# Hymba encoder layer, one core: neighbourhood attention in slots of two heads, with three score banks and three projection banks

## The chip, the cores and the metric

One core of a Trainium2 chip. The metric is the device time of one execution, in microseconds (us), from start to end on that core. The engines are TensorE (PE in the profile; PEld are its weight loads), VectorE (DVE), ScalarE (ACT), GpSimd (POOL) and SyncE (SP), which issues most of the transfers.

## What is computed

One layer over 1024 tokens (a grid of 16 rows by 64 columns) of width 1024, in float32. The kernel carries most operands of TensorE as a high and a low float16 part, so that three products stand for one in float32.

```python
x = rmsnorm(inp) * gain
qA,kA,vA,gateA, qB,kB,vB,gateB = split(x @ w_in)     # 1024 -> 3328
# group A: 8 query heads, 2 key/value heads of 64, normalised q and k, axial rotary, all 1024 keys
# group B: 8 heads of 64, neighbourhood attention over the grid:
#   window of 8 grid rows by 16 columns, clamped at the borders
sc = q @ k.T * 64**-0.5
sc = where(in_window, sc + bias[head, row offset, column offset], -inf)
p  = softmax(sc);  o = p @ v
mixed = concat(oA * silu(gateA), oB * silu(gateB))
out = rmsnorm(inp + mixed @ w_out) * gain_out
```

## The kernel before

The program runs in stages: the norm and the first projections, group A's attention, group B's attention (364.2 to 534.1), and the rest of the output projection. Projection work is cut into chunks of six matmuls of 128 x 128 by 128 x 256, and these chunks are laid between the matmuls of the attention, so that PE has work while the other engines do the softmax.

**Flow** sets the order. Its `step(n, first, second, last)` (L49 to L135) writes one slot: due ACT jobs; `first` (scores, bias, maximum, exponentials); `second` (low half); due DVE jobs; n chunks (`fill`, which carries fractions over); `last` (products with V). Jobs are the softmax's neighbours: reading out a projection's bank, splitting weights, splitting the mixed units, the final norm. Each has a delay counted in slots. A job runs in a slot if its engine's budget is not used up: us = base[0] + 0.654 n, for ACT us - base[1], for DVE us - base[2] (`BASE_B`). PE takes its instructions in program order, and so do all engines in group B's stage (`manual_schedule`).

**Group B** works on eight units u of 128 queries (order 0, 7, 1 to 6). Units 0 and 7 see 256 keys, the others 384. A slot is one head of one unit: 64 slots and 6 more to drain, with 2.4 chunks each.

- `b_scores` (L796) makes the scores of two heads at once, in every second slot, into two of four banks (two tiles of two banks each): L804 with the high part of q, L807 with the low part of k. It may append the sum of squares of a weight (`prep_b`, L366), whose four matmuls wait for the squares of ACT (L350).
- `b_qk` (L813): on DVE a custom instruction adds the bias and takes the row maximum (L825 and its accumulator read), a second one turns that into the exponent's bias (L827). On ACT the exponential is taken twice, to float32 (L828) and to float16 (L829).
- `b_lo` (L832), a slot later: DVE subtracts the two (L834), and SP issues one transpose (L838) of the high and low half, four or six blocks of 128 x 128.
- `b_pv` (L841), five slots after the scores (six from slot 40): three matmuls per key block, L851 to L853. After every fourth head the result is normalised (L860 to L863) and multiplied into the mixed activations on POOL (L865).

**Beside it** run: the last projections (tiles `pj`, read out by tanh on ACT, L682, and DVE, L687); the raw output weights 13 to 16, each 1 MB, loaded (L207), squared (L350), summed (L366 to L369) and split into high (L392) and low (L397) quarters; `os_start` (L875), which normalises a finished unit and splits it (L888 to L904), and its transposes (L913); the loads of the residual x (L951); and `out_gen` (L953), the output projection (tiles `po`, L482), added to x by DVE (L961). `fin_a` and `fin_b` (L978 to L994) do the last norm and store. Projections take turns in two PSUM tiles of one bank each. A weight that is not ready when its first chunk is written is forced by `need_w` (L433).

After the last V, the chunks left over run without softmax between them, and the last unit's projection (96 matmuls) ends the program.

Of the kernel before, what the change touches and what calls it, by code (L numbers as in the profile page):

```python
# [34 lines left out]
PREP = {2: 4, 3: 0, 4: 2}  # L35
NEG = -1.0e38
EPS = 1e-6
# [3 lines left out]
SLOTS = {"both": (16384, 2048, 4), "qc": (24576, 2048, 2), "stg1": (28672, 2048, 3), "stg": (18432, 2048, 3),  # L41
         "t": (0, 1536, 5), "ptb": (7680, 1536, 5), "ob": (15360, 1024, 1), "th": (16384, 16512, 2), "tha": (32896, 2048, 1), "y": (16384, 2048, 1),
         "p32": (AREA + 14464, 1536, 2)}
ORDER = (0, 7, 1, 2, 3, 4, 5, 6)
# [94 lines left out]
def kernel(ctx: ExitStack, tc: tile.TileContext, x: bass.AP, w: bass.AP, wo: bass.AP,  # L139
# [171 lines left out]


    def proj_tile(name):
        return ps_p.tile([P, 2, GC], F32, tag="pj", name=name)

# [27 lines left out]
    def squares(g, delay):  # L343

        wss[g] = [tn(f"wss{g}_{k}", 1, "ws") for k in range(4)]

        def quarter(i):
            o = (carve(ar, 16384 + SLOTS["th"][0] + (0 if "six" in late else (turn.get("th", 0) + 1) % 2) * SLOTS["th"][1], [512], BF16)
                 if "b" in late else va_more)
            act.activation(o.rearrange("p (k c) -> p k c", c=GC), raw[g][:, QUARTERS[i]], AF.Square, accum_out=wss[g][i])  # L350
# [328 lines left out]
    def g_gen(g, up, mix, cols, isb):  # L679
        def evac(pt):  # L680
            th = slot("th" if "b" in late else "tha", [P, 2, GC], F32)
            job("act", 0.7, lambda: act.activation(th, pt, AF.Tanh, scale=col(G2 + g - GATE)), late=0)  # L682
            m = mix[up][:, :, cols]

            def mul():
                if isb:
                    dve.scalar_tensor_tensor(m, th, 1.0, pt, op0=OP.add, op1=OP.mult)  # L687
# [94 lines left out]

    banks = []
# [28 lines left out]

    def b_qk(i, u, h):  # L813
        hh, h4i = divmod(h, 4)
        a, n = keys(u)
        w = n * P
        if h % 2 == 0:
            b_scores(u, (h, h + 1))
        s = sbs.pop((u, h))
        t, p32 = slot("t", [P, w], F32), slot("p32", [P, w], F32)  # L820
        hl = t.bitcast(F16).rearrange("p (a b) -> p a b", a=2)
        assert ("bias", int(0 < u < NU - 1), hh, h4i) in ready
        b = bias[hh][:, h4i, (a - u + 1) * P:(a - u + 1 + n) * P]
        mx = tn(f"mx{u}_{h}")
        dve.tensor_tensor_reduce(out=t, in0=s, in1=b, scale=1.0, scalar=-3e38,  # L825
                                 op0=OP.add, op1=OP.max, accum_out=mx)
        dve.tensor_scalar(mx, mx, col(NSB + hh), LN_P, op0=OP.mult, op1=OP.add)  # L827
        act.activation(p32, t, AF.Exp, bias=mx, scale=col(SCB + hh))  # L828
        act.activation(hl[:, 0], t, AF.Exp, bias=mx, scale=col(SCB + hh))  # L829
        hls["b", u, h] = (hl, p32)  # L830

    def b_lo(i, u, h):  # L832
        hl, t = hls.pop(("b", u, h))
        dve.tensor_tensor(hl[:, 1], t, hl[:, 0], op=OP.subtract)  # L834
        k = i - MORE + 5
        pt = (area(32896, [2 * keys(u)[1], P], F16) if k >= 0 and k % 6 == 5 else
              slot("ptb", [P, 2 * keys(u)[1], P], F16))
        sp.dma_start_transpose(pt, hl.rearrange("p a b -> p (a b)"))  # L838
        pts["b", u, h] = pt

    def b_pv(i, u, h):  # L841
        hh = h // 4
# [5 lines left out]
        o = pv["b", u, hh][:, h % 4]  # L848
        pt = pts.pop(("b", u, h))
        for c in range(n):  # L850
            pe.matmul(o, pt[:, c], vb[hh][:, a + c, h % 4, v_hi], start=c == 0, stop=False)  # L851
            pe.matmul(o[:, :D], pt[:, c], vb[hh][:, a + c, h % 4, v_lo], start=False, stop=False)
            pe.matmul(o, pt[:, n + c], vb[hh][:, a + c, h % 4, v_hi], start=False, stop=c == n - 1)  # L853
        if h % 4 == 3:
            def evac():
# [5 lines left out]
                dve.tensor_tensor(s4, s4, col(VF + 4 * hh, 4), op=OP.mult)  # L861
                ot = slot("ob", [P, 4, D], F32)
                dve.tensor_tensor(ot, pv["b", u, hh][:, :, :D], s4[:, :, None].to_broadcast([P, 4, D]), op=OP.mult)  # L863
# [11 lines left out]
    def os_start(u):  # L875
# [15 lines left out]
        def scale():  # L891
# [4 lines left out]
            for i in range(2):  # L896
                job("act", 0.72, hi, i, delay=1 + i, late=0, key=("os", u))

# [11 lines left out]
    def os_c(u):  # L910
        mT[u] = [m.bitcast(F16).rearrange("p (a b) -> p a b", b=P) for m in mixed(u)]
        for k in range(2):
            sp.dma_start_transpose(mT[u][k], osp[u][k])  # L913
        at(2, "end", turn_x2, u)

# [14 lines left out]
    def in_turn(fn, *a):  # L930

        lane.append((fn, a))
        if len(lane) == 1:
            fn(*a)
            at(2, "end", next_load)

    def next_load():
        lane.pop(0)
        if lane:
            lane[0][0](*lane[0][1])  # L940
            at(2, "end", next_load)

# [10 lines left out]
    def out_gen(jobs, done=()):  # L953
# [13 lines left out]
        for i, (u, g) in enumerate(jobs):  # L967
            need_w(g)
            fl.need(("os", u), lambda: u in mT)
            dve.tensor_tensor(rw[:, i:i + 1], rws[u][:, 3:4], col(RC + g), op=OP.mult)  # L970
            hi, lo = wp[g]
# [116 lines left out]

    def run_units(units, skew, qk, lo, pvf, n, hooks=None, by_hand=0, more=1000):

        m, hand = len(units), ExitStack()
        for i in range(m + skew + (more < 1000)):
            back = skew + (i >= more)
            if i == by_hand:
                hand.enter_context(tc.manual_schedule(engines={e.engine for e in (act, dve, pool, sp)}))
            first = (lambda: qk(i, *units[i])) if i < m else None
            second = (lambda: lo(i - 1, *units[i - 1])) if 1 <= i <= m else None
            last = (lambda: pvf(i - back, *units[i - back])) if i >= back and i != more else None
            if qk is a_qk:
                first, last = (lambda f=first, l=last: [g() for g in (f, l) if g]), None  # L1100
            if hooks:
                hooks(i)
            fl.step(n(i), first, second, last)
            sums_now()
# [10 lines left out]
    fl.base = BASE_A  # L1115
    with run_units(ua, SKEW_A, a_qk, a_lo, a_pv, rates(FILL_A + [(64 - n_head, mid)], FILL_A_END), by_hand=HAND):
        pass
# [11 lines left out]

    ub = [(u, h) for u in ORDER for h in range(NH)]  # L1130

    late["b"] = True
    def hooks(i):
        if i == 0:
# [4 lines left out]
            for h in range(4):  # L1139
                job("dve", 0.5, make, h, delay=h, late=0)  # L1140
        if i == 1:
            prep(13)
        if NH < i <= 2 * NH:
            at(1, "post", narrow, i - NH - 1)
        if i == 46:
            late["gout"] = one.tile([P, 1024], F32, tag="gain", name="gain_o")
# [18 lines left out]
    def hooks2(i):  # L1165
        hooks(i)
        if i == MORE - 2:
            late["six"] = True
        for u, k in zip(ORDER, SPLIT_AT):
            if i - SKEW_B - (i >= MORE) == k:  # L1170
                at(1, "post", os_start, u)

    for u in ORDER[4:7]:
        fl.add(*out_row(u))
    fl.base = BASE_B
    with run_units(ub, SKEW_B, b_qk, b_lo, b_pv, rates(FILL_B, FILL_B_END), hooks2, more=MORE):
        pass
# [92 lines left out]
```

## Time and profile before

| | us |
|---|---|
| median of 3 runs | 570.27 (569.89 to 574.81) |
| the profiled execution | 570.1 |
| its span | 568.3 |
| first matmul of group B's scores | 364.15 |
| first chunk after the last product with V | 534.07 |
| PE busy | 514.6 (91% of the span) |

The span is from the first to the last instruction. In a row of the timeline stand the start, the duration, engine, line, operation, what it writes and reads, shapes, and in brackets how long the engine idled before it and what ended the wait. A run of equal instructions is one row with a count. In a row of the groups stand the busy time and the mean duration in ns, then the idle time before them.

### The profile page before, as it was taken

The numbers are of one execution on the slowest core, as the hardware profiler recorded it, in microseconds if no ns is written. First come the engines' busy times: TensorE is split into PE (matmuls) and PEld (weight loads), VectorE is DVE, ScalarE is ACT, GpSimd is POOL, SyncE is SP. The second block draws the span as 40 slices with busy tenths as digits, with TensorE's granted clock in tenths as the row PEclk, the third lists the DMA queues.
The fourth block names the chain that finished last, engine by engine and source line by source line (L and its number), as shares of the span: only waits on it lengthen the run. The fifth ranks groups of instructions, "written<-read, shape, count | busy, mean of one in ns | idle before, by whom it ended". The sixth has DMA issues, their size and how long they took to land. (4 is left out here: it accounts for less than half of the span.)

```text
span 568.3 us, 13956 instructions
## 1 busy us (share of the span) xinstructions
PE 514.6 (91%) x5583; PEld 401.5 (71%) x5583; DVE 458.2 (81%) x1018; ACT 392.0 (69%) x615; POOL 152.0 (27%) x181
## 2 busy tenths in 40 slices
PE   2678989989999999999999999999798869997994
PEld 0456877868886555578888888887686647876883
DVE  4689788989887969788699888589978978988852
ACT  5546457857969769595776867397798978875321
POOL 2395887760000000000000024333611211212210
PEclk9979999999999999999999999999999979999998
DMA  8999547889999999998999989236647999899942
GB/s 240 217 181 232 121 84 195 140 141 181 224 223 179 186 214 189 220 172 177 224 164 191 194 175 190 89 66 122 151 97 131 222 170 156 143 175 170 190 110 74
DMA packets 245539, 95.49 MB, mean 168 GB/s; under 512 B 236513, under 2 KB 237025, under 8 KB 243554
## 3 DMA queue, kind: packets, MB, share of 16 engines
q1 hardware_dynamic: 241874, 73.89, 73.0%
q0 software_dynamic: 3312, 19.92, 12.4%
q8 instruction: 43, 0.70, 0.5%
q10 hardware_dynamic: 288, 0.79, 0.5%
q14 instruction: 22, 0.18, 0.1%
HBM read 29.56 MB, written 4.19 MB: 59 GB/s over the span
## 5 line engine op out<-in xcount | busy, mean ns | idle before, releaser
L482 PE MATMUL pj<-whl,hT 128*128 128x256 f16 x2112 | 254.2, 278 | 24.3 <-DMA hT<-ar 7.3
L482 PEld LDWEIGHTS <-hT 128*128 128x128 f16 x2112 | 203.8, 99 | 61.6 <-issue 19.9
L722 ACT ACTIVATE ar<-s,nm,sm 128x1024 f32<-128x1024 f32 x64 | 76.9, 1202 | 55.1 <-DVE nm L720 53.5
L720 DVE CUSTOM_DVE_ANT_0 ar<-s,sm 128x1024 bf16<-128x1024 f32 x64 | 81.9, 1280 | 32.5 <-PE s L715 32.2
L482 PEld LDWEIGHTS <-ar 128*128 128x128 f16 x768 | 73.1, 99 | 15.5 <-issue 6.6
L728 DVE TENSOR_TENSOR ar<-ar 128x1024 f16<-128x1024 f32 x64 | 79.4, 1241 | 1.4 <-ACT ar L723 1.4
L482 PE MATMUL po<-whl,ar 128*128 128x256 f16 x576 | 69.9, 276 | 1.8 <-DVE x2b L961 1.5
L723 ACT ACTIVATE ar<-ar 128x1024 f16<-128x1024 f32 x64 | 67.6, 1057 | 2.1 <-DVE sum L752 0.3
L828 ACT ACTIVATE rq<-ar,mx,sm 128x384 f32<-128x384 f32 (+1 forms) x64 | 43.1, 673 | 28.5 <-DVE mx L827 28.3
L829 ACT ACTIVATE ar<-ar,mx,sm 128x384 f16<-128x384 f32 (+1 forms) x64 | 43.5, 680 | 2.1
L482 PE MATMUL kb<-hT,whl 128*128 128x512 f16 x192 | 44.5, 379 | 0.0
L834 DVE TENSOR_TENSOR ar<-rq,ar 128x384 f16<-128x384 f32 (+1 forms) x64 | 35.5, 554 | 8.1 <-ACT ar L829 7.9
L746 PE MATMUL pv<-va,ar 128*128 128x64 f16 x384 | 40.0, 194 | 0.0
L745 PE MATMUL pv<-va,ar 128*128 128x65 f16 x384 | 39.9, 193 | 0.0
L747 PE MATMUL pv<-va,ar 128*128 128x65 f16 x384 | 39.8, 192 | 0.0
L397 DVE SCALAR_TENSOR_TENSOR whl<-raw,sm,whl 128x512 f16<-128x512 f32 x52 | 39.5, 789 | 0.0
L745 PEld LDWEIGHTS <-ar 128*128 128x128 f16 x384 | 35.5, 96 | 5.3
L746 PEld LDWEIGHTS <-ar 128*128 128x128 f16 x384 | 35.3, 97 | 5.3
L713 PE MATMUL s<-kTa,rq 128*128 128x512 f16 x128 | 38.1, 379 | 0.0
L207 POOL DMA_DIRECT2D raw<-in_w_dram x11 | 6.7, 607 | 111.2 <-ACT ar L723 89.0
L747 PEld LDWEIGHTS <-ar 128*128 128x128 f16 x384 | 35.4, 99 | 0.0
L392 ACT ACTIVATE whl<-raw,sm 128x512 f16<-128x512 f32 x52 | 33.9, 709 | 1.4 <-POOL sm L369 1.4
(163 smaller groups left out, 918.1 us busy)
## 6 DMA issues: line engine op xcount, KB each, us to landing
raw<-in_w_dram POOLq DMA_DIRECT2D x11, 1024.0 KB, 7.5
raw<-in_wo_dram POOLq DMA_DIRECT2D x4, 1024.0 KB, 5.6
ar<-in_x_dram SPq DMA_DIRECT2D x7, 512.0 KB, 6.5
khh<-ar SPq DMA_DIRECT2D x16, 128.0 KB, 3.4
x2b<-in_x_dram POOLq DMA_DIRECT2D x4, 512.0 KB, 5.7
x<-in_x_dram POOLq DMA_DIRECT2D x4, 512.0 KB, 5.8
out_dram<-x2b SPq DMA_DIRECT2D x8, 256.0 KB, 4.9
ar<-ar SPq DMA_TRANSPOSE x112, 4.5
```

Of the source, the lines that this page charges most:

```text
L397: dve.scalar_tensor_tensor(wp[g][1][:, q], raw[g][:, q], col(S_ + g), wp[g][0][:, q], op0=OP.mult, op1=OP.subtract)
L482: pe.matmul(*o[0], **o[1])
L713: pe.matmul(s[:, c * 512:(c + 1) * 512], q, kTa[:, 4 * c:4 * c + 4, hh], start=True, stop=False)
L720: dve.tensor_tensor_reduce(out=hl[:, 1].bitcast(BF16), in0=s, in1=col(SHA).to_broadcast([P, 1024]), scale=col(NSA), scalar=3e38, op0=OP.ad ...
L722: act.activation(p32, s, AF.Exp, bias=nm, scale=col(SCA))
L723: at(0, "mid", lambda: act.activation(hl[:, 0], p32, AF.Copy))
L728: dve.tensor_tensor(hl[:, 1], p32, hl[:, 0], op=OP.subtract)
L745: pe.matmul(o, pt[:, kt], va[:, kt, hh, v_hi], start=kt == 0, stop=False)
L746: pe.matmul(o[:, :D], pt[:, kt], va[:, kt, hh, v_lo], start=False, stop=False)
L747: pe.matmul(o, pt[:, 8 + kt], va[:, kt, hh, v_hi], start=False, stop=kt == 7)
L828: act.activation(p32, t, AF.Exp, bias=mx, scale=col(SCB + hh))
L829: act.activation(hl[:, 0], t, AF.Exp, bias=mx, scale=col(SCB + hh))
```

## The change

- Group B's slot is now a unit and a pair of heads: 32 slots and 3 to drain (`SKEW_B` 3), with 4.2 chunks each in place of 2.4 (35 x 4.2 = 147 chunks, where 70 x 2.4 = 168 stood). The rest of the chunks comes after the last V.
- DVE's instruction multiplies by a negative scale and takes the minimum (L829), so its result is the exponent's bias and the step of L827 goes. ACT takes each exponential once (L831), for both heads side by side, and one copy scaled by 2^14 makes the high half of the pair (L833, 512 or 768 columns). DVE makes the pair's low half in one instruction (L838), and one transpose (L840) takes the pair's 8 or 12 blocks.
- The low half of the pair before now comes ahead of the slot's scores' reduction. The ring for DVE's output has three buffers of a pair (five of a head), the float32 exponentials one (two), the transposed ones three (five).
- Scores take turns in three banks. The fourth, which is the second half of the tile whose first half is score bank 2, becomes a third bank for projections (`proj_tile`).
- Delays of some jobs are shortened (`at(2, ..)` to `at(1, ..)`, `os_start` in the slot itself, both quarters of L907 one slot after); the scratch for squares moves; the row weight `rw` for two output columns is made in one instruction where both are ready.

Core of the diff:

```diff
-BASE_A, BASE_B = (1.8, 2.6, 2.9), (0.8, 0.9, 1.0)
+BASE_A, BASE_B = (1.8, 2.6, 2.9), (1.7, 2.1, 2.4)
-SKEW_A, SKEW_B = 5, 5
+SKEW_A, SKEW_B = 5, 3
-FILL_B_END = 2.4
-MORE = 40
-SPLIT_AT = (8, 16, 24, 32, 40, 48, 56)
+FILL_B_END = 4.2
+SPLIT_AT = (4, 8, 12, 16, 20, 24, 28)
-NEG = -1.0e38
+NEG = -1.0e37
-         "t": (0, 1536, 5), "ptb": (7680, 1536, 5), "ob": (15360, 1024, 1), ...
-         "p32": (AREA + 14464, 1536, 2)}
+         "t": (0, 3072, 3), "ptb": (9216, 3072, 3), "th": (32896, 2048, 1), "y": (32896, 2048, 1),
+         "p32": (AREA + 14464, 3072, 1)}
...
     def proj_tile(name):
-        return ps_p.tile([P, 2, GC], F32, tag="pj", name=name)
+        if not banks:
+            return ps_p.tile([P, 2, GC], F32, tag="pj", name=name)
+        if not own:
+            own.extend(ps_p.tile([P, 2, GC], F32, tag="pj", name=f"pjb{i}") for i in range(2))
+            own.append(banks[3].rearrange("p (a b) -> p a b", b=GC))
+        k = turn["own"] = turn.get("own", -1) + 1
+        return own[k % 3]
...
-        return banks[k % 4 if kind == "sb" else 4 + k % 2]
+        return banks[k % 3 if kind == "sb" else 4 + k % 2]
...
-    def b_qk(i, u, h):
+    def b_qk(u, p):
...
+        b_scores(u, (2 * p, 2 * p + 1))
+        t, p32 = slot("t", [P, 2, w], F32), slot("p32", [P, 2, w], F32)
+        hl = t.rearrange("p e k -> p (e k)").bitcast(F16).rearrange("p (a k) -> p a k", a=2)
+        for e in range(2):
...
+            dve.tensor_tensor_reduce(out=t[:, e], in0=sbs.pop((u, h)), in1=b, scale=col(NSB + hh), scalar=3e38,
+                                     op0=OP.add, op1=OP.min, accum_out=nm)
+            act.activation(p32[:, e], t[:, e], AF.Exp, bias=nm, scale=-1.0)
+        p32 = p32.rearrange("p e k -> p (e k)")
+        act.activation(hl[:, 0], p32, AF.Copy, scale=2.0 ** 14)
-        dve.tensor_tensor_reduce(out=t, in0=s, in1=b, scale=1.0, scalar=-3e38,
-                                 op0=OP.add, op1=OP.max, accum_out=mx)
-        dve.tensor_scalar(mx, mx, col(NSB + hh), LN_P, op0=OP.mult, op1=OP.add)
-        act.activation(p32, t, AF.Exp, bias=mx, scale=col(SCB + hh))
-        act.activation(hl[:, 0], t, AF.Exp, bias=mx, scale=col(SCB + hh))
...
+    def b_lo(u, p):
+        hl, p32 = hls.pop(("b", u, p))
+        dve.scalar_tensor_tensor(hl[:, 1], p32, 2.0 ** 14, hl[:, 0], op0=OP.mult, op1=OP.subtract)
+        pt = slot("ptb", [P, 4 * keys(u)[1], P], F16)
+        sp.dma_start_transpose(pt, hl.rearrange("p a k -> p (a k)"))
...
+    def parts_b(i, back):
+        def first():
+            if 1 <= i <= 32:
+                b_lo(*ub[i - 1])
+            if i < 32:
+                b_qk(*ub[i])
+        return first, None, (lambda: b_pv(*ub[i - back])) if i >= back else None
```

Three places in the built order. First DVE, at the turn from a unit of 256 keys to one of 384. `sb` are score banks, `pvb` the products with V, `mx` and `nm` the maximum and the negated one, ISA the custom instruction and its read. Before:

```order
L825 ISA ar,mx_0_5653<-sb_5107,ar 128x384
L825 ISA mx_0_5653 128x1
L827 TENSOR_SCALAR mx_0_5653<-mx_0_5653,sm 128x1
L834 TENSOR_TENSOR ar<-rq,ar 128x256
L904 SCALAR_TENSOR_TENSOR mhl_5586<-ar,os_5585,mhl_5586 128x512
L825 ISA ar,mx_1_5683<-sb_5107,ar 128x384
L825 ISA mx_1_5683 128x1
L827 TENSOR_SCALAR mx_1_5683<-mx_1_5683,sm 128x1
L834 TENSOR_TENSOR ar<-rq,ar 128x384
```

And now:

```order
L838 SCALAR_TENSOR_TENSOR ar<-rq,ar 128x512
L829 ISA ar,nm_0_5549<-sb_5107,ar,sm 128x384
L829 ISA nm_0_5549 128x1
L829 ISA ar,nm_1_5552<-sb_5108,ar,sm 128x384
L829 ISA nm_1_5552 128x1
L693 SCALAR_TENSOR_TENSOR ar<-ar,sb_5108 128x2x256
L403 SCALAR_TENSOR_TENSOR rest_5102<-raw_5039,sm,rest_5101 128x512
L838 SCALAR_TENSOR_TENSOR ar<-rq,ar 128x768
```

The low half moved ahead of both reductions, the step on `mx` is gone, and L693 reads a projection out of the tile `sb_5108`, from which L829 reads scores too.

Second PE, at the start of a pair slot in which the third projection bank is next. `khh` and `klo` are the keys, `qTb` the queries, `whl` a projection weight, `hT` the normalised input; 5107 is the tile of score banks 0 and 1, 5108 that of score bank 2 and the third projection bank. In brackets is the engine that a matmul waits for. Before, with projections in a tile of their own:

```order
L366 MATMUL sb_5107<-wss_2_5615,mh 128x1 [waits Activation_49]
L366 LDWEIGHTS mh
L366 MATMUL sb_5107<-wss_3_5616,mh 128x1 [waits Activation_49]
L482 LDWEIGHTS hT_99
L482 MATMUL pj_2_5913<-whl_4862,hT_99 128x256
```

And now:

```order
L808 MATMUL sb_5108<-khh,qTb_106 128x384
L808 LDWEIGHTS qTb_106
L808 MATMUL sb_5107<-khh,qTb_106 128x384 [waits DVE_49]
L811 LDWEIGHTS qTb_106
L811 MATMUL sb_5108<-klo,qTb_106 128x384
L811 LDWEIGHTS qTb_106
L811 MATMUL sb_5107<-klo,qTb_106 128x384
L488 LDWEIGHTS hT_99
L488 MATMUL sb_5108<-whl_4862,hT_99 128x256 [waits DVE_49]
```

The chunk right behind the scores writes the tile of a score bank that has just been filled, and waits for DVE.

Third ACT, where output weight 15 is squared and split. `raw` is the weight, `wss` the sums of squares, `mhl` the split of a mixed unit. Before:

```order
L350 ACTIVATE ar,wss_3_5616<-raw_5611 128x512
L828 ACTIVATE rq<-ar,mx_5_5827,sm 128x384
L829 ACTIVATE ar<-ar,mx_5_5827,sm 128x384
...
L828 ACTIVATE rq<-ar,mx_1_6289,sm 128x384
L829 ACTIVATE ar<-ar,mx_1_6289,sm 128x384
L392 ACTIVATE whl_6306<-raw_5611,sm 128x512 x2
```

And now:

```order
L356 ACTIVATE rest_5101,wss_2_6324<-raw_6320 128x512
L831 ACTIVATE rq<-ar,nm_0_6601 128x384
L831 ACTIVATE rq<-ar,nm_1_6604 128x384
L833 ACTIVATE ar<-rq 128x768
L356 ACTIVATE rest_5101,wss_3_6325<-raw_6320 128x512
L907 ACTIVATE mhl_6548<-ar,os_6547 128x512 x2
L398 ACTIVATE whl_6641<-raw_6320,sm 128x512 x4
```

Before, some 40 instructions of ACT lie between the fourth square and the first high quarter of the weight; now two do. The fourth square itself stands behind the exponentials and the copy of a slot.

More of the change, by code (lines that the diff above doesn't have):

```diff
@@ L969, in out_gen @@
             fl.need(("os", u), lambda: u in mT)
-            dve.tensor_tensor(rw[:, i:i + 1], rws[u][:, 3:4], col(RC + g), op=OP.mult)
+            if i == 0 and jobs[-1] == (u, g + 1) and g + 1 in ready:
+                dve.tensor_tensor(rw, col(RC + g, 2), rws[u][:, 3:4].to_broadcast([P, 2]), op=OP.mult)
+            elif i == 0 or not both:
+                dve.tensor_tensor(rw[:, i:i + 1], rws[u][:, 3:4], col(RC + g), op=OP.mult)
+            both = i == 0 and jobs[-1] == (u, g + 1) and g + 1 in ready
             hi, lo = wp[g]
@@ L1087, with run_units @@
         mixA[up] = carve(ar, MIX + 4096 * up, [2, 512], F32)
[L1089 to L1093, printed above, removed]
+    def run_units(m, skew, parts, n, hooks=None, by_hand=0):
+        hand = ExitStack()
+        for i in range(m + skew):
             if i == by_hand:
                 hand.enter_context(tc.manual_schedule(engines={e.engine for e in (act, dve, pool, sp)}))
[L1096 to L1100, printed above, removed]
             if hooks:
                 hooks(i)
-            fl.step(n(i), first, second, last)
+            fl.step(n(i), *parts(i, skew))
             sums_now()
@@ L1139, in hooks @@
             for h in range(4):
-                job("dve", 0.5, make, h, delay=h, late=0)
+                job("dve", 0.5, make, h, delay=h // 2, late=0)
         if i == 1:
             prep(13)
-        if NH < i <= 2 * NH:
-            at(1, "post", narrow, i - NH - 1)
-        if i == 46:
+        if 4 < i <= 8:
+            for e in range(2):
+                at(1, "post", narrow, 2 * (i - 5) + e)
+        if i == 25:
             late["gout"] = one.tile([P, 1024], F32, tag="gain", name="gain_o")
```

76 lines of the change are left out of this document (36 added, 40 removed).

## The prediction

> **What bounds the kernel now.** I read the page's busy times first, then the timeline of the neighbourhood stage (group B), TensorE's waits in it, the windows, and last the groups of instructions.
>
> ```profile
> PE 514.6 (91%) x5583; PEld 401.5 (71%) x5583; DVE 458.2 (81%) x1018; ACT 392.0 (69%) x615; POOL 152.0 (27%) x181
> ```
>
> TensorE (PE) is the busiest, but an average hides which stage stalls. The change touches group B's stage and what comes after it, so I fix its two ends in the timeline of PE.
>
> ```profile
> 364.15 0.38 PE L804 MATMUL sb<-khh,qTb 128*128 128x256 f16 x2
> ...
> 533.80 0.19 PE L851 MATMUL pvb<-ar 128*128 128x65 f16 x1
> ...
> 534.07 4.75 PE L482 MATMUL po<-whl,ar 128*128 128x256 f16 x42
> 538.66 2.78 PE L482 MATMUL po<-rest,ar 128*128 128x256 f16 x24
> 541.28 8.02 PE L482 MATMUL po<-whl,ar 128*128 128x256 f16 x72
> 549.14 0.38 PE L482 MATMUL po<-rest,ar 128*128 128x256 f16 x2
> 549.98 2.56 PE L482 MATMUL po<-rest,ar 128*128 128x256 f16 x22 [0.46 <-DMA ar<-mhl]
> 552.37 8.02 PE L482 MATMUL po<-whl,ar 128*128 128x256 f16 x72
> ```
>
> The first scores start at 364.15 and the last product with V ends at 534.07: the loop takes 169.9 us. Then PE runs 42+24+72+2+22+72 = 234 matmuls of the output projection with one wait of 0.46, and the program ends at 568.3, 34.2 us after the last V. From 541.28 to 549.14 there are 72 of them: 0.109 us each. A head's nine matmuls with V take 534.07 - 533.80 = 0.27. Where does the loop lose time?
>
> ```profile
> PE pvb L851 <- DMA ar<-ar: 9.7, 5, 4.9
> PE pj L482 <- DVE ar L687: 4.4, 2, 2.9
> PE po L482 <- DVE x2b L961: 2.7, 2, 1.5
> PE sb L804 <- DVE mx L825: 0.4, 1, 0.4
> PE po L482 <- DVE x L961: 0.2, 1, 0.2
> ```
>
> These are PE's waits from 364 to 534.3 (total, times, longest): 17.4 us. The largest is V waiting for the transposed probabilities, the next two a projection chunk waiting until DVE has read out its bank. One wait costs more than itself. The windows (PE's busy time, then its granted clock) show it:
>
> ```profile
> 404.00:408.00 4.00, 1.41 (x16) 1.00 0.94 301
> ...
> 460.00:462.00 2.00, 1.48 (x14) 0.50 1.12 241
> 462.00:464.00 2.00, 2.00 (x12) 0.50 0.98 228
> 464.00:466.00 2.00, 2.00 (x24) 0.81 1.22 190
> ```
>
> Around 404 to 408 PE idles for 2.6 us and the clock stays 1.00. After the wait of 4.9 us that ends at 460.5 it is 0.50 until about 464.8 (0.81 in the last window is 0.38 of its 2 us at one half): 4.2 us of work at half speed, 2.1 us lost. So 17.4 + 2.1 = 19.5 us is what a perfect order could win in this loop, and 150.4 us of PE's work stays.
>
> **Part 1: fewer chunks in the loop.** Before, 70 slots take 2.4 chunks of six matmuls, 168; after, 35 take 4.2, 147. 21 x 6 = 126 matmuls move behind the last V: 126 x 0.109 = 13.8 us leave the loop and come back in the tail. They are not a pure loss: the tail's wait of 0.46 us goes, since the last unit's split and transposes (534.1 to 550.0, 15.9 us) now lie under 360 - 96 = 264 leftover matmuls, 28.8 us. Tail: 34.2 + 13.8 - 0.5 = 47.5. Loop without waits: 150.4 - 13.8 = 136.6.
>
> **Part 2: what a pair slot asks of each engine.** A slot before the chunks, and the work of DVE and ACT per head:
>
> ```profile
> 396.76 0.48 PE L804 MATMUL sb<-khh,qTb 128*128 128x384 f16 x2
> 397.17 0.34 PE L807 MATMUL sb<-klo,qTb 64*128 64x384 f16 x2
> 397.44 1.48 PE L482 MATMUL pj<-whl,hT 128*128 128x256 f16 x12
> ```
>
> ```profile
> L825 DVE CUSTOM_DVE_ANT_0 ar<-sb,rq 128x384 f32<-128x384 f32 x24 | 13.2, 549 | 3.1 <-DMA ar<-ar 3.1
> L825 DVE DVE_READ_ACCUMULATOR2_ANT mx<- 128x1 f32 x64 | 5.2, 81 | 0.0
> L827 DVE TENSOR_SCALAR mx<-mx,sm 128x1 f32<-128x1 f32 x64 | 13.7, 214 | 2.3
> L834 DVE TENSOR_TENSOR ar<-rq,ar 128x384 f16<-128x384 f32 x48 | 27.2, 566 | 4.8 <-ACT ar L829 4.8
> L828 ACT ACTIVATE rq<-ar,mx,sm 128x384 f32<-128x384 f32 x48 | 33.5, 699 | 21.8 <-DVE mx L827 21.7
> L829 ACT ACTIVATE ar<-ar,mx,sm 128x384 f16<-128x384 f32 x48 | 33.9, 707 | 1.6
> L392 ACT ACTIVATE whl<-raw,sm 128x512 f16<-128x512 f32 x16 | 10.5, 708 | 0.0
> L723 ACT ACTIVATE ar<-ar 128x1024 f16<-128x1024 f32 x64 | 67.6, 1057 | 2.1 <-DVE sum L752 0.3
> L397 DVE SCALAR_TENSOR_TENSOR whl<-raw,sm,whl 128x512 f16<-128x512 f32 x16 | 12.4, 807 | 0.0
> L350 ACT ACTIVATE ar<-raw 128x512 bf16<-128x512 f32 x16 | 9.9, 618 | 0.1
> L350 ACT ACTIVATION_READ_ACCUMULATOR ar<-raw 128x1 f32 x16 | 3.0, 187 | 0.0
> ```
>
> PE: scores 397.44 - 396.76 = 0.68, two heads of V 0.54, 24 to 30 chunk matmuls 2.6 to 3.3: 3.9 to 4.5 us. DVE: two reductions of 0.55 + 0.08, and one low half of 768 columns. The trace has no such instruction; below it stand the two of 384 (1.13) less one fixed part, above it one of 512 at 0.81 stretched by 768/512 (1.21). I take 0.95, nearer the old pair, in which the fixed part is paid twice. The L827 step goes: 64 x 0.214 = 13.7 us of DVE. ACT: two exponentials of 0.70 and a copy of 768 columns, between 0.71 (512 columns) and 1.06 (1024): 0.86, where two of 0.707 stood, a gain of 0.55 per pair, 17.7 us in all. Both gains lie beside PE and count nothing in the sum, but they are the cover for the rest: the slot gives DVE's other jobs 1.7 + 0.654 x 4.2 - 2.4 = 2.05 us, so DVE has 1.26 + 0.95 + 2.05 = 4.3 us a slot, level with PE; with the old steps it would be 1.26 + 0.43 + 1.13 + 2.05 = 4.9, and PE would wait 0.4 to 1 us in each of 32 slots.
>
> The low half and its transpose come first in the next slot. From there to V lie nearly three pair slots, 3 x 158.3/35 = 13.6 us less the work ahead (158.3 is the loop of the sum below), some 12, where there were four single ones, 4 x 169.9/70 = 9.7. So I take V's waits of 9.7 as gone, the clock's 2.1 with them, and the 7.3 on L687, L961 and L825 as replaced by Part 3. If V's waits stay, the sum is 9.7 higher; they can't bring more than they cost.
>
> **Part 3: a projection bank that shares its tile.** The third projection bank is the other half of the tile in which score bank 2 lies, and the built order makes the one wait for the readers of the other. Counted in that order, at five places the chunk right behind the scores waits for DVE's reduction of those scores. It can't begin before the scores are there, so PE stands for one to two reductions, 0.63 to 1.26, and longer when a job is ahead; 1.2 each, 6.0. At four places the scores wait until a projection in the neighbour half is read out:
>
> ```profile
> L682 ACT ACTIVATE ar<-pj,sm 128x512 f32<-128x512 f32 x11 | 7.4, 669 | 5.4 <-PE pj L482 5.4
> L687 DVE SCALAR_TENSOR_TENSOR ar<-ar,pj 128x512 f32<-128x512 f32 x8 | 5.5, 683 | 1.4 <-ACT ar L682 1.2
> ```
>
> 0.67 for the tanh, 0.68 more for DVE where the second reader is not done; 1.1 each, 4.4. Together 10.4. Behind such a chunk stand, on PE, the rest of the slot's chunks, an old pair's V and the next scores, so DVE's next reduction starts later by as much. The bounds: nothing, if DVE and ACT are ahead each time (the old wait on scores was 0.4, once), and 9 x 2.9 = 26, the longest wait on L687 now.
>
> **Part 4: output weights just in time.** Delays are counted in slots, and a slot is now twice as long, so the splits of the output weights 13 to 16 end close to their first chunk. Before, the sums of squares for 15 and 16 stand right behind scores, long ahead of use. Now, for 15, the fourth square stands on ACT behind the slot's two exponentials and copy, and behind it two splits of the mixed unit (L907, 0.71 each as L392), then the weight's high and DVE's low quarter. From the scores: 1.26 + 0.70 + 0.86 + 0.62 + 0.19 (the read of its accumulator) + 1.42 + 0.71 + 0.81 = 6.6 us (the sum over the squares and its power lie beside the 1.42); 18 chunk matmuls cover 2.0: wait 4.6. For 16 the square comes earlier but the high quarter still sits behind the slot's three: 1.26 + 0.70 + 0.86 + 1.42 + 0.71 + 0.81 = 5.8, covered by 12 matmuls, 1.3: wait 4.5. For 13 and 14 only the last low quarters are late, one to one and a half of L397: 1.3 and 0.9. Sum 11.3; bounds nothing (the splits done a slot sooner) and 4 x 4.9 = 20.
>
> **The sum.** 364.2 + 136.6 + 10.4 + 11.3 + 47.5 = 570.0 of span; the profiled execution took 570.1 for a span of 568.3, so 1.8 more: **571.8 us**. Its own before is 570.1, the median of the runs 570.27, so the two can be compared as they are. Faster by over 1% would be below 564.6, slower above 576.0; 1% is about what a measurement of this kernel tells from none.
>
> **Rivals.** *The shared tile costs nothing.* For it: DVE loses 13.7 us of L827 and PE waited on scores only once. Against it: the wait is in the order, and a reduction can't be ahead of its own scores. Then 571.8 - 10.4 = 561.4, faster.
>
> *The two weight waits halve the clock.* The one wait of 4.9 did it (0.50 above), 2.6 idle did not. At 4.6 and 4.5 both may: 2 x 2.1 = 4.2, so 576.0. The Trainium skill, "TensorE: Matmul & The Clock Gate", Part 1 (The HAM clock gate), has a rule for it: a free-running window of about 3.4 us without work drops the clock to half, and about as long of work brings it back. The trace agrees: 4.9 idle, then 4.3 at one half. By that rule a wait of 4.6 holds a whole window (4.6 - 3.4)/3.4 = one time in three, an estimate, and the time would be 571.8 + 0.35 x 4.2 = 573.3.
>
> *Transposes land too late; slower than before.* Each pair is now one transpose of 12 blocks where a head's had 6, and the ring behind DVE's reductions has three buffers: the reduction of a pair overwrites what the transpose of three pairs ago reads. That transpose is issued about two slots ahead, 8 us. Landings of the old ones, a head's (mostly 6 blocks) and group A's (16 blocks), from the views of their lines L838 and L733:
>
> ```profile
> DMA to landing us min/median/max: 2.4/3.0/9.5
> ```
>
> ```profile
> DMA to landing us min/median/max: 4.2/5.0/8.2
> ```
>
> The medians give (5.0 - 3.0)/10 = 0.2 us per block, 4.2 for 12: in time. But the longest, 9.5 + 6 x 0.2 = 10.7, is 2.7 past it, and the four loads of x and the raw weights 15 and 16 now fall in the same five slots. From a landing of 8 us this decides. Five such waits, as many as V had for its transposes, make 13.5: 585.3.
>
> **How the numbers follow.** Forecast (571.8) 0.40, its own range 566 to 577; shared tile free (561.4) 0.35; clock (576.0) 0.10; late transposes (585.3) 0.15. Faster by over 1%: the 0.35 and 0.02 of the forecast's edge, 0.37. Slower: 0.03 of that edge, half of the clock's, nearly all of the last: 0.22. Same: 0.41. The range runs from 557, a little below the first rival since part of the weights' 11.3 may also vanish, to 585.
>
> **What would show it.** Right: the last V near 522.5 (364.2 + 158.3), then 360 projection matmuls with no wait; PE waits on DVE's score reduction from projection chunks, some 10 us; two waits of over 4 us on the weights 15 and 16; low half near 0.95 and copy near 0.86. Wrong: no wait from a chunk on a reduction (first rival); clock at 0.50 behind the weights' waits (second); DVE reductions waiting for a DMA, more than the 3.1 us in L825's row (third); or V still waiting some 10 us for transposes, which would fell Part 2.

## The result and the profile after

The changed kernel takes 595.2 us (median of 4 runs, 594.3 to 596.5) where the one before took 571.0 in the same series: ratio 1.041, interval 1.036 to 1.047. The forecast was 571.8, no change; it is slower by 24 us, outside the range. The profiled execution has a span of 594.7.

The two ends of group B's loop in PE's timeline:

```profile
366.26 0.38 PE L808 MATMUL sb<-khh,qTb 128*128 128x256 f16 x2
...
547.59 0.19 PE L860 MATMUL pvb<-ar 128*128 128x65 f16 x1
547.62 0.60 PE L488 MATMUL sb<-whl,ar 128*128 128x256 f16 x4
```

The loop takes 547.6 - 366.3 = 181.4 us, where it took 169.9 and was to take 158.3. The tail is 594.7 - 547.6 = 47.1; forecast 47.5. So the whole miss lies in the loop, but for 2.1 us by which it starts later. The tail's wait of 0.46 us is gone, as forecast. PE's waits in the loop (total, times, longest):

```profile
PE sb L488 <- DVE nm L829: 22.8, 8, 8.4
PE sb L488 <- ACT whl L398: 5.0, 1, 5.0
PE pjb L488 <- ACT whl L398: 1.7, 1, 1.7
PE pvb L372 <- ACT rest L356: 1.7, 2, 1.3
PE pjb L488 <- DVE rest L403: 1.6, 1, 1.6
PE pjb L488 <- DVE whl L403: 1.0, 2, 0.6
PE sb L488 <- DVE whl L403: 0.4, 1, 0.4
PE sb L808 <- DVE nm L829: 0.4, 1, 0.4
PE sb L808 <- ACT ar L688: 0.2, 1, 0.2
```

No V waits for a transpose any more. The first row is the shared tile: a projection chunk into `sb` waits for a reduction of scores. With the last two rows, in which scores wait for a score bank, it is 23.4 us; the six rows between them, on weights (L398, L403 and the squares L356), make 11.4. Together 34.8. The granted clock (third number) behind the longest waits:

```profile
396.00:398.00 2.00, 2.00 (x11) 0.50 0.74 135
...
445.20:452.00 6.80, 6.80 (x53) 0.66 0.66 138
484.20:490.00 5.80, 5.80 (x50) 0.73 0.71 128
490.00:500.00 10.00, 6.64 (x54) 0.71 0.43 102
...
519.30:526.00 6.70, 5.03 (x35) 0.58 0.20 39
```

Of 181.4 us PE is busy for 146.6 and waits for 34.8. Taken window by window (2 us each, busy time times what the clock falls short of 1.00), 10.7 of the busy time is lost to the clock, of which 2.3 in the second row (6.80 x 0.34) and 2.1 in the last. That leaves 135.9 of work at full clock, where 136.6 was forecast.

Why is a reduction 7 or 8 us late? Around 445, in order of time on ACT, DVE and PE:

```profile
438.00 0.63 ACT L895 ACTIVATE mhl<-ar 128x512 bf16<-128x512 f32 x1 [4.70 <-DMA ar<-mhl]
...
438.63 2.54 ACT L398 ACTIVATE whl<-raw,sm 128x512 f16<-128x512 f32 x4
...
443.09 0.96 DVE L838 SCALAR_TENSOR_TENSOR ar<-rq,ar 128x768 f16<-128x768 f32 x1 [3.39 <-ACT ar L833]
...
445.18 1.22 PE L488 MATMUL sb<-whl,hT 128*128 128x256 f16 x5 [6.97 <-DVE nm L829]
```

ACT is to square a mixed unit into a buffer that a transpose of the unit before still reads, and waits 4.7 us. Behind the square stand four high quarters of a weight (2.54), then the slot's exponentials and copy, DVE's low half behind the copy, the reduction behind the low half, and through the shared tile PE's chunk behind that. Around 484 it is a transpose:

```profile
467.81 6.55 SPq L840 DMA_TRANSPOSE ar<-ar  x1
...
482.97 0.62 DVE L829 CUSTOM_DVE_ANT_0 ar<-sb,rq,sm 128x384 f32<-128x384 f32 x1 [6.15 <-DMA ar<-ar]
...
484.19 2.08 PE L488 MATMUL sb<-rest,ar 128*128 128x256 f16 x9 [8.45 <-DVE nm L829]
```

The reduction waits 6.15 us for a buffer of the ring of three that a transpose still reads: the one issued at 467.81, by the order of the ring, which let it go only 15 us later. The two pairs' transposes before it, issued at 455.2 and 461.3, landed after 6.3 and 11.5 us, where those from 380 to 454 took 3.0 to 5.0. That comes when six loads, 4 MB, are issued within 17 us (POOL's timeline):

```profile
388.10 0.64 POOL L206 DMA_DIRECT2D raw<-in_wo_dram  x1 [1.80 <-DVE sm L420]
454.39 0.60 POOL L958 DMA_DIRECT2D x2b<-in_x_dram  x1 [6.61 <-PE sb L488]
459.88 0.58 POOL L958 DMA_DIRECT2D x2b<-in_x_dram  x1
460.44 0.58 POOL L206 DMA_DIRECT2D raw<-in_wo_dram  x1
465.00 0.55 POOL L958 DMA_DIRECT2D x2b<-in_x_dram  x1
467.17 0.56 POOL L206 DMA_DIRECT2D raw<-in_wo_dram  x1 [1.61 <-ACT mhl L907]
471.61 0.58 POOL L958 DMA_DIRECT2D x2b<-in_x_dram  x1
```

The `raw` rows after 388 are weights 15 and 16. Before the change they were issued at 402 and 437:

```profile
401.99 0.59 POOL L207 DMA_DIRECT2D raw<-in_wo_dram  x1
437.49 0.62 POOL L207 DMA_DIRECT2D raw<-in_wo_dram  x1 [8.50 <-issue]
```

The new instructions were priced about right (groups, mean ns behind the busy time):

```profile
L829 DVE CUSTOM_DVE_ANT_0 ar<-sb,rq,sm 128x384 f32<-128x384 f32 x24 | 13.8, 614 | 11.9 <-DMA ar<-ar 6.2 <-PE sb L811 5.7
L838 DVE SCALAR_TENSOR_TENSOR ar<-rq,ar 128x768 f16<-128x768 f32 x24 | 23.6, 985 | 12.0 <-ACT ar L833 11.9
L833 ACT ACTIVATE ar<-rq 128x768 f16<-128x768 f32 x24 | 20.2, 843 | 0.8
L831 ACT ACTIVATE rq<-ar,nm 128x384 f32<-128x384 f32 x48 | 27.0, 607 | 46.6 <-DVE nm L829 46.6
```

Low half 0.985 (0.95), copy 0.843 (0.86), exponential 0.607 (0.70); the reduction grew from 0.55 to 0.61. A pair's transpose landed after 3.0 us at least, 3.7 in the median and 11.5 at the longest (4.2 and 10.7 worked out for the last two).

### The profile page after: what moved, and what is told of

It is laid out like the page before. It is cut to its first block, busy times and chain, and to the rows that moved or that the text cites. A ratio compares the mean times of both kernels' runs of the same rounds, so it can differ in the third digit from the quotient of the medians.

```text
span 594.7 us, 13779 instructions
## 1 busy us (share of the span) xinstructions
PE 523.3 (88%) x5583; PEld 406.3 (68%) x5583; DVE 447.2 (75%) x911; ACT 369.2 (62%) x583; POOL 155.1 (26%) x181
## 4 chain that ended last, share of the span: by engine, by line
PE 58%; DVE 7%; ACT 5%; DMA 5%; issue 4%; SPq 0%; POOL 0%; DVEq 0%; POOLq 0%; ACTq 0%
PE pj L488 18%; PE pjb L488 7%; PE kb L488 7%; PE sb L488 6%; DMA ar<-ar 4%; PE s L719 4%; PE s L721 4%; DVE ar L829 3%; PE pv L752 3%; PE pv L753 2%; PE pv L751 2%; ACT rq L831 2%; ACT ar L833 1%; DVE whl L403 1%; PE sb L808 1%
## 5 line engine op out<-in xcount | busy, mean ns | idle before, releaser
L488 PEld LDWEIGHTS <-hT 128*128 128x128 f16 x2112 | 206.2, 100 | 72.4 <-issue 27.8
L488 PE MATMUL pj<-whl,hT 128*128 128x256 f16 x1680 | 201.9, 278 | 20.8 <-ACT whl L381 7.7
L488 PEld LDWEIGHTS <-ar 128*128 128x128 f16 x768 | 75.8, 100 | 36.5 <-issue 23.1
L831 ACT ACTIVATE rq<-ar,nm 128x384 f32<-128x384 f32 (+1 forms) x64 | 34.2, 580 | 55.1 <-DVE nm L829 54.5
L488 PE MATMUL pjb<-whl,ar 128*128 128x256 f16 x408 | 49.3, 278 | 2.7 <-ACT whl L398 1.7
L838 DVE SCALAR_TENSOR_TENSOR ar<-rq,ar 128x768 f16<-128x768 f32 (+1 forms) x32 | 29.8, 933 | 15.7 <-ACT ar L833 15.6
L403 DVE SCALAR_TENSOR_TENSOR whl<-raw,sm,whl 128x512 f16<-128x512 f32 x52 | 39.1, 790 | 2.9 <-ACT whl L398 2.9
L751 PEld LDWEIGHTS <-ar 128*128 128x128 f16 x384 | 35.6, 97 | 5.5 <-issue 0.3
L872 POOL TENSOR_TENSOR ar<-ar,qkg 128x256 f32<-128x256 f32 x16 | 18.4, 1149 | 80.4 <-DVE qkg L870 65.6
L752 PEld LDWEIGHTS <-ar 128*128 128x128 f16 x384 | 35.4, 97 | 5.5 <-issue 0.3
L753 PEld LDWEIGHTS <-ar 128*128 128x128 f16 x384 | 35.5, 99 | 0.0
L398 ACT ACTIVATE whl<-raw,sm 128x512 f16<-128x512 f32 x52 | 33.7, 708 | 1.4 <-POOL sm L375 1.4
```

Source lines behind the costliest of these rows:

```text
L398: act.activation(wp[g][0][:, q], raw[g][:, q], AF.Copy, scale=col(S_ + g))
L403: dve.scalar_tensor_tensor(wp[g][1][:, q], raw[g][:, q], col(S_ + g), wp[g][0][:, q], op0=OP.mult, op1=OP.subtract)
L488: pe.matmul(*o[0], **o[1])
L751: pe.matmul(o, pt[:, kt], va[:, kt, hh, v_hi], start=kt == 0, stop=False)
L752: pe.matmul(o[:, :D], pt[:, kt], va[:, kt, hh, v_lo], start=False, stop=False)
L753: pe.matmul(o, pt[:, 8 + kt], va[:, kt, hh, v_hi], start=False, stop=kt == 7)
```

## The experiments

Each group of kernels ran on one chip beside the kernel before the change; times are medians, ratios are to that kernel with their 95% interval. Three explanations stood against each other: S, the shared tile; W, late weights; C (later C2), that chunks taken out of the loop leave holes in it rather than shorten it. L is that the late feeders would show elsewhere without the tile, P that DVE and ACT have no room in the loop.

**Two score banks**, so that no tile is shared:

```diff
-        return banks[k % 3 if kind == "sb" else 4 + k % 2]
+        return banks[k % 2 if kind == "sb" else 4 + k % 2]
```

> The changed kernel with scores taking turns in two banks (the one tile of two) and the third projection bank kept: no score bank and no projection bank share a tile any more. The changed kernel takes 595.2 us; in its trace PE waits 23.5 us in group B's loop for reductions through the shared tile, 0.9 to 8.4 each, and the granted clock is low behind the long ones, some 6 us of work lost. Theory S (the shared tile turns every delay of DVE into a wait of PE): the 23.5 and the 6 go, 566 us. Theory L (late feeders: ACT waited 4.7 us for a transposed mixed unit, DVE 6.2 for a transpose; the tile only shows it): the two long waits come back as waits of the next scores or of V, only the small ones (8 us) go, 585 to 587 us.

593.7 us (586.0 to 596.6 in four runs); the ratio 1.029 (1.020 to 1.037) is of the lower two. That is L (585 to 587 would be 1.025 to 1.028), not S: in the profiled execution, the longest of the four, the shared tile's waits became

```profile
PE pvb L858 <- DMA ar<-ar: 10.8, 1, 10.8
PE sb L808 <- DVE nm L829: 5.6, 2, 4.0
PE pvb L372 <- ACT rest L356: 4.8, 5, 2.3
PE sb L488 <- ACT whl L398: 4.7, 1, 4.7
...
```

one wait of V of 10.8 us for a late transpose, and 18.2 on the weights in place of 11.4. The loop stays at 181.7.

**Four score banks and two projection banks**, the old division:

```diff
-            own.append(banks[3].rearrange("p (a b) -> p a b", b=GC))
...
-        return own[k % 3]
+        return own[k % 2]
...
-        return banks[k % 3 if kind == "sb" else 4 + k % 2]
+        return banks[k % 4 if kind == "sb" else 4 + k % 2]
```

> The changed kernel with four score banks and two projection banks, as before the change: no shared tile, but no third projection bank either. Theory S: 23.5 and 6 us go, waits of a projection chunk for its bank come back as before the change (7.3 us), 573 us. Theory L: 585 us or more, the two long waits now on a projection bank, on scores or on V.

584.5 us, ratio 1.021 (1.017 to 1.024): between the two. Of its 26 us of waits 23 are on weights 13 to 16, among them one of 8.0 on the last low quarter of 13. Here too ACT waits 4.56 us (until 435.18) for the buffer of the mixed unit, but PE waits for no more than 0.2 us between 397 and 453: without the tile that delay does not reach it. The shared tile alone does not explain the loss.

**One part alone on the old kernel: the arithmetic.**

```diff
-NEG = -1.0e38
+NEG = -1.0e37
...
-        dve.tensor_tensor_reduce(out=t, in0=s, in1=b, scale=1.0, scalar=-3e38,
-                                 op0=OP.add, op1=OP.max, accum_out=mx)
-        dve.tensor_scalar(mx, mx, col(NSB + hh), LN_P, op0=OP.mult, op1=OP.add)
-        act.activation(p32, t, AF.Exp, bias=mx, scale=col(SCB + hh))
-        act.activation(hl[:, 0], t, AF.Exp, bias=mx, scale=col(SCB + hh))
+        dve.tensor_tensor_reduce(out=t, in0=s, in1=b, scale=col(NSB + hh), scalar=3e38,
+                                 op0=OP.add, op1=OP.min, accum_out=mx)
+        act.activation(p32, t, AF.Exp, bias=mx, scale=-1.0)
+        act.activation(hl[:, 0], p32, AF.Copy, scale=2.0 ** 14)
...
-        dve.tensor_tensor(hl[:, 1], t, hl[:, 0], op=OP.subtract)
+        dve.scalar_tensor_tensor(hl[:, 1], t, 2.0 ** 14, hl[:, 0], op0=OP.mult, op1=OP.subtract)
```

> The kernel before the change, one part alone: the minimum of the negated scores in one instruction, one exponential and one scaled copy, head by head. It saves 64 x 0.21 us of DVE. Theories S and L both: no cause of the loss, 566 to 571 us. Rival A (the new arithmetic lengthens the chain, 0.61 in place of 0.55 per reduction and a copy that must wait for the exponential): over 575 us.

559.9 us, ratio 0.977 (0.973 to 0.982): faster than the kernel before, and more than expected. The loop falls from 169.9 to 159.3, since PE's waits halve, 17.4 to 8.7 us. The run does not tell what DVE's lost step gives from what ACT's cheaper exponentials give.

**One part alone: fewer chunks.**

```diff
-FILL_B_END = 2.4
+FILL_B_END = 2.1
```

> The kernel before the change, one part alone: 2.1 chunks per slot in place of 2.4 (147 in the loop). Theories S and L: 126 matmuls move behind the last V, the loop gets shorter by about as much, 568 to 574 us. Rival C (the loop of 170 us goes at the pace of DVE and ACT, so that chunks taken out of it leave holes): the loop stays 165 us or more and the time rises to 580 to 585 us.

594.2 us, ratio 1.038 (1.032 to 1.045): beyond even rival C (580 to 585). This number alone makes the old kernel as slow as the changed one. The tail grows as reckoned, 34.2 to 47.8, but the loop does not shrink, it grows to 182.8:

```profile
PE pvb L851 <- DMA ar<-ar: 11.6, 4, 7.9
PE po L482 <- DVE whl L397: 7.1, 4, 5.3
PE po L482 <- ACT whl L392: 6.9, 1, 6.9
PE po L482 <- DVE rest L397: 4.6, 3, 3.4
PE pj L482 <- DVE whl L397: 3.2, 1, 3.2
```

21.8 us of waits on weights (splits L392 and L397), and V's for transposes.

**The budget.** A slot's budget for jobs is counted from its chunks; in the built order weight 13 is fully split after 79 of 128 heads (64 of group A and 64 of group B) before the change, after 104 in the changed kernel and 103 with 2.1 chunks. In the traces its last low quarter starts at 399.7, 458.6 and 453.1 us. The raw weight 15 is loaded into what 13 gives free. So the next kernel changes only the number from which the budgets are counted:

```diff
-BASE_A, BASE_B = (1.8, 2.6, 2.9), (1.7, 2.1, 2.4)
+BASE_A, BASE_B = (1.8, 2.6, 2.9), (2.1, 2.1, 2.4)
```

> The changed kernel (595.2 us) with one number changed: the slot's time from which the budgets of other jobs are counted is 2.1 + 0.654 n in place of 1.7 + 0.654 n, so DVE's jobs get 2.45 us a slot in place of 2.05; the 4.2 chunks stay. In the built order the last low quarter of output weight 13 moves from behind 104 of 128 reductions to behind 80 (79 before the change), and with it the load of raw weight 15. Theory W (fewer chunks shrink the budget, the weights' splits starve, weights 13 to 16 and 4 MB of loads come late and together): the waits on weights fall from 11.4 to under 5 us, the wait on a late transpose (8.4) and most of the clock's loss go, 568 to 575 us. Rival P (DVE and ACT have no room in the loop; more jobs per slot only lengthen it): waits on the reduction grow, 590 us or more.

576.9 us, ratio 1.009 (1.006 to 1.011): 18 us of the 24 are gone. Raw weight 15 is loaded early again,

```profile
403.34 0.62 POOL L206 DMA_DIRECT2D raw<-in_wo_dram  x1
```

PE waits on no weight, and the loop is 161.9, 19.5 shorter: 13.7 of that are waits and 5.3 the clock. It is just above W's figure. The wait of 8.4 on the late transpose is gone as expected, but the one of 7 us behind ACT's buffer stays (7.1, at 447.4), chunks now wait elsewhere for reductions, and the shared tile still makes 21.1 us of waits, all that is left.

**4.8 chunks**, as many in the loop as before:

```diff
-FILL_B_END = 4.2
+FILL_B_END = 4.8
```

> The changed kernel with 4.8 chunks per slot (168 in the loop, as before the change), which also gives DVE's jobs 2.45 us a slot. Theory W: as with the larger budget, and 126 matmuls cover the loop again, 562 to 568 us, the tail 33 to 34 us. Rival P: the loop stays at 180 us, 582 us.

580.1 us, ratio 1.013 (1.008 to 1.017), against W's figure and close to P's: no wait on weights, tail 34.1, but the loop stays at 180.1, with 17.7 us of waits of chunks on reductions. W alone does not carry it either; P falls with the kernel of both causes undone, below.

**The old kernel with 2.1 chunks and its budgets restored:**

```diff
-BASE_A, BASE_B = (1.8, 2.6, 2.9), (0.8, 0.9, 1.0)
+BASE_A, BASE_B = (1.8, 2.6, 2.9), (1.0, 0.9, 1.0)
...
-FILL_B_END = 2.4
+FILL_B_END = 2.1
```

> The kernel before the change with 2.1 chunks per slot (594.2 us alone) and the budgets of the jobs as they are at 2.4 chunks (base 1.0 in place of 0.8). Theory W: weight 13 is split at 93 heads in place of 103, the waits on weights of 27 us mostly go, 572 to 580 us. Rival P: no gain, 590 us or more.

583.8 us, ratio 1.017 (1.012 to 1.022); between the two figures. Waits on weights fall from 21.8 (not the 27 of the expectation) to 3.1, but V's on transposes rise from 11.6 to 17.4, and the loop is 170.3, as long as with 2.4 chunks.

**Both causes undone: 4.8 chunks and no shared tile** (two_pj_banks, and):

```diff
-FILL_B_END = 4.2
+FILL_B_END = 4.8
```

> The changed kernel with 4.8 chunks per slot and no shared tile (four score banks, two projection banks; 584.5 us with 4.2 chunks). Theory W and S together: neither late weights nor the shared tile, 556 to 562 us, faster than before the change. Rival P: 575 us or more.

557.7 us, ratio 0.976 (0.970 to 0.982), as expected: faster than both kernels, level with the arithmetic alone. Its loop is 156.8 us with 7.5 of waits, and its clock in it 1.00.

**The larger budget, no shared tile, but 4.2 chunks** (two_pj_banks, and):

```diff
-BASE_A, BASE_B = (1.8, 2.6, 2.9), (1.7, 2.1, 2.4)
+BASE_A, BASE_B = (1.8, 2.6, 2.9), (2.1, 2.1, 2.4)
```

> The changed kernel with 4.2 chunks, no shared tile (four score banks, two projection banks) and the larger budget of jobs (2.1 in place of 1.7). The two causes found so far are both undone while the 126 matmuls stay behind the last V. If W and S are all there is, the loop is 136.6 us of PE's work and some 8 us of waits, the tail 47, in all 556 to 562 us, level with 4.8 chunks (557.7). Rival C2 (the moved chunks are missed as cover even with early weights): the loop stays at 157 to 162 us, 570 to 576 us.

571.5 us, ratio 1.000 (0.996 to 1.004): rival C2, not W with S. Its loop, below that of the kernel with 4.8 chunks (length, PE's busy time, granted clock):

```profile
362.88:519.67 156.79, 149.24 (x1686) 1.00 0.83 160
366.74:523.55 156.81, 139.73 (x1561) 0.97 0.76 148
```

156.8 us, to the tenth what 4.8 chunks take, with 126 matmuls (13.8 us) fewer in it. In their place stand 16.9 us of waits where 7.5 were, and the clock loses 3.9 where it lost nothing:

```profile
PE pvb L857 <- DMA ar<-ar: 8.6, 3, 4.5
PE pvb L857 <- DVE qkg L869: 4.3, 4, 2.8
PE pjb L487 <- DVE x2b L967: 1.8, 2, 1.6
PE pjb L487 <- DVE ar L692: 1.4, 1, 1.4
...
```

In the second row V waits for its bank (`qkg` is the scratch into which V's result is normalised). That read-out waits for a gate's projection, which comes later with fewer chunks per slot; at 4.8 chunks the row is not there.

**Still fewer chunks, 3.9,** with the budgets of the last kernel:

```diff
-BASE_A, BASE_B = (1.8, 2.6, 2.9), (2.1, 2.1, 2.4)
+BASE_A, BASE_B = (1.8, 2.6, 2.9), (2.3, 2.1, 2.4)
...
-FILL_B_END = 4.2
+FILL_B_END = 3.9
```

In this kernel the gates come so late that one half unit's V result is read only after its bank was written again; that part of the output differs, the instructions are the same.

> The kernel of budget_two_pj (4.2 chunks, no shared tile; 571.5 us, its loop 156.8 us with 17 us of waits) with 3.9 chunks per slot and the same 4.85 us a slot to count the jobs' budgets from. 63 more matmuls, 6.9 us, move behind the last V. Theory C2 (without shared tile and late weights the loop still goes at some 157 us, the pace of the pairs' chain and the jobs on DVE and ACT, and chunks taken out of it leave holes): the loop stays 154 to 160 us, the tail grows to 54, 576 to 581 us. Rival C (the loop follows PE's work): the loop falls to 150 us, 569 to 573 us.

576.5 us, ratio 1.008 (1.005 to 1.012), C2: the loop takes 157.2 and the tail 54.4.

```profile
368.71:525.91 157.20, 137.40 (x1494) 0.93 0.77 148
```

**4.8 chunks with two score banks and three projection banks** (two_score_banks, and):

```diff
-FILL_B_END = 4.2
+FILL_B_END = 4.8
```

> The changed kernel with 4.8 chunks, two score banks and three projection banks of which none shares a tile with scores. By S, level with four score and two projection banks (557.7 us) or better by the 4.5 us that chunks still waited for their bank there: 552 to 558 us. Rival L2 (two score banks tie PE to the reduction of the pair before, as its waits of 5.6 us at 4.2 chunks showed): 565 us or more.

561.5 us (554.9 to 564.9 in its runs), ratio 0.978 (0.969 to 0.986): between S and L2, and not to be told from two projection banks. An unshared third bank brings nothing that these runs can show. This kernel has fewer score banks than the change, and as many projection banks, and can't be told from the one with four and two. So, at 4.8 chunks, it is the sharing of the tile that costs, not the number of banks.

**One part alone on the old kernel: the shared bank,** with `proj_tile` as in the change and

```diff
-        return banks[k % 4 if kind == "sb" else 4 + k % 2]
+        return banks[k % 3 if kind == "sb" else 4 + k % 2]
```

> The kernel before the change, one part alone: three score banks, and the fourth as a third projection bank in the same tile as score bank 2. By S PE now waits through the shared tile for DVE's reductions, 10 to 20 us with some lost clock, against 7.3 us of waits for a projection bank that go: 575 to 590 us. Rival: in slots of one head the reduction is early enough, 565 to 571 us.

581.1 us, ratio 1.016 (1.010 to 1.022), by S: 7.3 us of waits for a projection bank and 9.0 of V's go, and these come:

```profile
PE sb L490 <- DVE mx L831: 11.5, 8, 3.1
PE sb L810 <- DVE mx L831: 7.8, 6, 3.1
...
```

The second row is scores waiting for a score bank, so part of the loss may lie in having three of them in place of four.

## Why the prediction was wrong

The pieces in one table (median us):

| | shared tile | no shared tile |
|---|---|---|
| 4.2 chunks | 595.2 (the change) | 584.5 |
| 4.2 chunks, larger budget | 576.9 | 571.5 |
| 4.8 chunks | 580.1 | 557.7 |

- **Part 1 failed: "13.8 us leave the loop and come back in the tail."** They came back (47.1 of 47.5 forecast), and PE's work did fall as forecast (135.9 of 136.6), but the loop did not get shorter by it. Without shared tile and late weights it divides like this (us, the lost clock summed as in the result):

| chunks | work at full clock | lost clock | PE idle | loop |
|---|---|---|---|---|
| 4.8 | 149.2 | 0.0 | 7.6 | 156.8 |
| 4.2 | 135.8 | 3.9 | 17.1 | 156.8 |
| 3.9 | 128.4 | 9.0 | 19.8 | 157.2 |

  I took PE's work out and kept the old waits' list, when the right question was what else in the loop would be late next. The runs name three things: transposes, the gates that free V's banks, and the splits, whose budget shrinks with the chunks. The bare price is 571.5 - 557.7 = 13.8 us, all of the moved work; with the shrunk budget 584.5 - 557.7 = 26.8. In the changed kernel itself PE's idle time is all in waits on the tile and on weights (23.4 + 11.4 = 34.8).
- **Part 3 had the mechanism and too small a size:** 23.4 us, not 10.4. Forecast were five waits of chunks and four of scores, 1.1 or 1.2 us each; measured are eight of chunks, 22.8 us in all, and next to none of scores. I priced a wait as one or two reductions. The tile passes on whatever the reduction itself waits for: 4.7 us of ACT on a buffer (with 2.5 of splits behind it) and 6.15 of DVE on a transpose stand behind the two longest, 7.0 and 8.4. With 4.8 chunks the tile costs 580.1 - 557.7 = 22.3, with 4.2 and the larger budget 5.4, on the old kernel alone 9.2 (581.1 less the 571.9 beside it). In the row of the change it shows as 10.7. It costs less where other waits take its place.
- **Part 4 was right in the sum,** 11.4 against 11.3 us, with luck: for weights 13 to 16 the waits are 1.6, 0.6, 3.4 and 5.8, forecast 1.3, 0.9, 4.6 and 4.5. It was wrong in its weight: I treated the late splits as four separate waits. They also hold back the loads of weights 15 and 16, so that 4 MB come together when transposes are needed. Raising the budget alone took 18 us off. That the loads make the transposes late is argued from their coming together; no run moved the loads alone.
- **The clock** was a rival with 4.2 us at two waits; it is 10.7 us, behind five falls to one half.
- **Late transposes**, the rival on the slower side, came true in its place and by its ring of three buffers, twice (8.6 us of DVE's idle time). The first reached PE, through the shared tile, as the wait of 8.4.
- **Part 2 held in its prices, and by luck in the rest.** The new instructions cost what was worked out, and no V waits for a transpose in the changed kernel. But there the loop is 181 us long. In the kernel with the larger budget and two projection banks, whose loop of 156.8 is the nearest to the 158.3 that I reckoned with, V waits 8.6 us for transposes again; the cover of 12 us was not always enough at that pace with 4.2 chunks. And the two gains I counted at nothing ("lie beside PE") are worth 11 us on the old kernel, as the arithmetic alone. Work off the critical path was setting PE's waits.

In sums: the forecast's 571.8, plus 13.0 for the tile, 10.7 for the clock, 0.1 for the weights, 2.1 of a later start, less 0.7 of PE's work and 0.4 of tail, gives 596.6, the profiled execution's time (594.7 and some 1.8 around it). From the old kernel, in this order: the arithmetic -11.1, pairs with the old number of chunks and banks -2.2 (not to be told from nothing), the shared tile +22.3, fewer chunks with their budget +15.2; together +24.2 (medians of several series, whose kernel before lay between 571.0 and 573.5). In another order the last two come out otherwise, as the table shows.

Left open: what sets the 157 us at 4.2 and 3.9 chunks. DVE is busy 129 of 158 us at 4.2, so it isn't full, and each kernel shows another mixture of waits. Nor was it tried to give the mixed units a second buffer, which the wait of 4.7 us asks for, or to spread the loads.

## What to carry to other kernels

Here the work that fills the loop on the busiest engine also sets the schedule of the other jobs. Before such work is moved out, ask which jobs, loads and bank releases are counted from it, and measure the loop with the work gone (on the old kernel one number, 2.1 for 2.4, made a loss as large as the whole change). A bank that shares a tile with another use ties the two users together where dependencies are kept by tile. The price is then the slowest thing that either waits for, not one instruction. A saving on an engine that is off the critical path is not worth nothing if the bound engine's waits end on it.

## What the runs showed of the hardware

The clock fell to one half after shorter waits than the one of 4.9 us from which I priced it. In the changed kernel

```profile
395.34 1.01 PE L488 MATMUL sb<-whl,hT 128*128 128x256 f16 x4 [2.44 <-DVE nm L829]
```

a wait of 2.44 us that ends at 395.3 (with 0.4 shortly ahead) is followed by 0.50 from 396 to 398 (the first window row of the result). Before the change one of 2.9, which ends at 408.3, left it at 1.00, and so did one of 2.8, which ends at 397.25, in the kernel with the larger budget and two projection banks:

```profile
396.00:398.00 2.00, 0.75 (x14) 1.00 0.61 118
398.00:400.00 2.00, 2.00 (x19) 1.00 0.11 21
```

So the length of a single wait does not decide it. The Trainium skill, "TensorE: Matmul & The Clock Gate", Part 1 (The HAM clock gate), says that the window of about 3.4 us runs freely. That agrees with a length that does not decide; but a window of that size with no work at all cannot have fitted into 2.44 us.

DVE's reduction of 384 columns took 0.61 us with the scale from a column and the minimum, and 0.55 with a constant and the maximum. Which of the two makes the difference was not tried.

The first score came between 362.9 and 368.7 us in the variants of the changed kernel, whose program up to there is the same, so differences of a few us in one profile are not to be read.
